# Half of the Strassen activation sums on GpSimd, and one plain tile fewer in the second half layer

## The chip, the cores and the metric

The kernel runs on one core of one Trainium2 chip. Its time is the device time of one launch in microseconds (us). A run of the kernel before and one of the changed kernel can be told apart from about 0.2% on, some 3.3 us here.

The engines are named as in the profile: PE is the matrix engine (TensorE), PEld its weight loads, DVE the vector engine (VectorE), ACT the scalar engine (ScalarE), POOL is GpSimd, SP the sync engine, which issues most loads. Each engine works through its own queue of instructions strictly in order, and waits for others at semaphores.

## The reference

One step of a two-layer decoder, in float32, for 512 prompt tokens and 8 sample tokens that share the weights (520 token columns in all), with a model width of 1024 and a feed-forward width of 2816. The first layer mixes tokens with a pooling mixer, the second with windowed attention; around each mixer stand two feed-forward blocks that add half of their output:

```python
def _rmsnorm(x, g):
    y = xf * lax.rsqrt(jnp.mean(xf * xf, axis=-1, keepdims=True) + EPS)
    return (y * g.astype(jnp.float32)).astype(x.dtype)

def _swiglu(x, wg, wu, wd):
    return (jax.nn.silu(x @ wg) * (x @ wu)) @ wd

# every layer: x += 0.5*SwiGLU(rms(x)); x += mixer(rms(x)); x += 0.5*SwiGLU(rms(x))
```

So there are four feed-forward blocks. They are called half layers here and numbered fi = 0 to 3.

## The kernel before

The residual stream lies transposed in SBUF: eight tiles x0 to x7 of 128 model rows by 520 token columns. Every float32 product is formed of three fp32r products (high times high, low times high, high times low), so each weight and each activation is first split into a high and a low part: ACT copies the high part (`wh`, `th`), DVE subtracts it to get the low part (`wl`, `tl`). The token columns are worked in two halves of 260.

A half layer has 22 tiles of 128 hidden columns. Each tile needs gate and up products. A **plain** tile takes 96 matmuls of 128x260 (8 row blocks, 2 weights, 2 halves, 3 products). A **Strassen** tile uses seven block products instead of eight, 84 matmuls; it needs sums of weight blocks and sums of activation blocks. `NPL` says how many tiles of each half layer are plain; they come first and give the sums time to be formed.

The activation sums are formed once for each half layer. For quarter k = 0 to 3, ACT writes the scaled inputs `xa` (from x_k) and `xb` (from x_k+4), in slots of tag "sa". Then four sums of 128x260 are formed on DVE: t1 = b11 - b12, t2 = -t1 - b22, t3 = b22 - b12, t4 = -t2 - b21. t1 and t2 fill the tile `t12`, t3 and t4 the tile `t34` (tag "sb", which other values share). Both tiles are then split: ACT writes `th` (L358), DVE writes `tl` (L359). In fi = 0 and 2 this is the generator `sums()` (L676, L677, L681, L682), and the order of its instructions among the others is set by the framework's scheduler. In fi = 1 and 3 it is `begin()` (t1 to t4 at L839, L841, L843, L845, the splits at L852), and the order is set by the planner `Steps`, which is given an engine, a cost in us and a due time for each step, and the slots that it takes. There t1 to t4 are the steps T{k}1 to T{k}4, the splits H{k}0 and L{k}0 (of t12), H{k}1 and L{k}1 (of t34). The first Strassen product s0 needs no sums; the second, s1, needs all four L{k}0.

The weight sums are two. SP loads a chunk `raw` (1 MB, gate then up, at L372) and one more block into a tile `S`. POOL then issues two accumulating DMAs on its own queue (L157 into `S`, L158 within `raw`), each of which waits until its loads have landed. DVE adds twice more (L163, L167). A chunk slot is loaded again as soon as its last block has been split (L196, L225).

POOL otherwise computes little: the power step of the norm in `begin()` (L805, N.r in the plan), parts of the attention softmax (L1856, L1817), and some DMAs of results.

At the start of each half layer the norm is computed beside the first plain tiles. In fi = 0, ACT squares the eight x tiles into `sq` and DVE adds them into `acc` (L1088); PE sums acc over the rows (L498); DVE computes the reciprocal root `r_tok` by Newton steps (L506 to L513); PE spreads it over the columns (L519, L522); ACT copies it to `R` (L523, L524). The gate values of the plain tiles are multiplied by R afterwards. In fi = 1 and 3 the same steps are N.s (L798), N.m (L802, DVE), N.r (L805, POOL), N.b (L810, L813, PE) and copies at L819.

Of the kernel before, what the change touches and what calls it, by code (L numbers as in the profile page):

```python
# [15 lines left out]
ALU = mybir.AluOpType  # L16
# [11 lines left out]
PARTS = (8, 8, 6)  # L28
LAG = 2
VLAG = 3  # L30
NPL = (3, 3, 2, 2)
HD = 64
NB = SP // P
WINS = (2, 4, 8, 16)
# [211 lines left out]
class Steps:  # L246
# [8 lines left out]
    def add(self, name, eng, cost, due, fn=None, after=(), takes=(), reads=()):  # L255
        self.steps[name] = (eng, cost, due, fn, tuple(after), tuple(takes))
        for key in reads:
            self.readers.setdefault(key, []).append(name)
# [58 lines left out]
def yoco_step(ctx, tc, ins, outs):  # L317
    nc = tc.nc
# [3 lines left out]
    V, S, T = nc.vector, nc.scalar, nc.tensor  # L322
# [41 lines left out]
    def later(ins):  # L364

        return tc.keep_in_program_order(ins)
# [297 lines left out]
    def sums(tmp, n, tt):  # L664


        for k in range(4):
            xa = tmp.tile([P, TOK], F32, tag="sa", name="xa")
            xb = tmp.tile([P, TOK], F32, tag="sa", name="xb")
            for kk, xn in ((k, xa), (k + 4, xb)):  # L670
                S.activation(xn, x[kk], AF.Copy, scale=gcol(n, kk))
            t12 = tmp.tile([P, TOK], F32, tag="sb", name="t12", bufs=nsb[0])
            t34 = tmp.tile([P, TOK], F32, tag="sb", name="t34", bufs=nsb[0])
            b11, b12, b21, b22 = hcols(xa, 0), hcols(xa, 1), hcols(xb, 0), hcols(xb, 1)
            t1, t2, t3, t4 = hcols(t12, 0), hcols(t12, 1), hcols(t34, 0), hcols(t34, 1)
            later(V.tensor_tensor(t1, b11, b12, op=ALU.subtract))  # L676
            V.scalar_tensor_tensor(t2, t1, -1.0, b22, op0=ALU.mult, op1=ALU.subtract)  # L677
            tt[k] = pair(TT, [P, TOK])
            split(tt[k], t12)
            yield  # L680
            later(V.tensor_tensor(t3, b22, b12, op=ALU.subtract))  # L681
            V.scalar_tensor_tensor(t4, t2, -1.0, b21, op0=ALU.mult, op1=ALU.subtract)  # L682
            tt[k + 4] = pair(TT, [P, TOK])
            split(tt[k + 4], t34)
            yield
# [99 lines left out]
    def begin(st, fi, n, mov, tmp, tt, first, off, base, need, ready, summed, hidden_list, root_):  # L785


        add, vals = st.add, {}
# [32 lines left out]
        d = base + root_  # L821
# [11 lines left out]
        def t_sum(k, i):  # L833
            (b11, b12), (b21, b22) = ((hcols(vals["X", k, a], 0), hcols(vals["X", k, a], 1)) if ("X", k, a) in vals else (None, None) for a in range(2))
            if i in (1, 3):
                vals["t", k, i // 2] = tmp.tile([P, TOK], F32, tag="sb", name="t12" if i == 1 else "t34", bufs=nsb[0])
            h = lambda j: hcols(vals["t", k, (j - 1) // 2], (j - 1) % 2)
            if i == 1:
                V.tensor_tensor(h(1), b11, b12, op=ALU.subtract)  # L839
            elif i == 2:  # L840
                V.scalar_tensor_tensor(h(2), h(1), -1.0, b22, op0=ALU.mult, op1=ALU.subtract)  # L841
            elif i == 3:
                V.tensor_tensor(h(3), b22, b12, op=ALU.subtract)  # L843
            else:
                V.scalar_tensor_tensor(h(4), h(2), -1.0, b21, op0=ALU.mult, op1=ALU.subtract)  # L845

# [7 lines left out]
        for k in range(4):  # L854
            d = S0 - 14.0 + 3.0 * k
            add(f"X{k}0", "ACT", 0.72, d, lambda k=k: scaled(k, 0), after=ready(k) + ([f"X{k - 1}1"] if k else []), takes=("sa",))
            add(f"X{k}1", "ACT", 0.72, d, lambda k=k: scaled(k, 1), after=ready(k + 4) + [f"X{k}0"], takes=("sa",))
            x0, x1 = ("sa", f"X{k}0"), ("sa", f"X{k}1")
            add(f"T{k}1", "DVE", 0.43, d + 0.5, lambda k=k: t_sum(k, 1), after=[f"X{k}0"], takes=("sb",), reads=[x0])
            add(f"T{k}2", "DVE", 0.43, d + 1.0, lambda k=k: t_sum(k, 2), after=[f"X{k}1", f"T{k}1"], reads=[x1])  # L860
            add(f"T{k}3", "DVE", 0.43, d + 1.1, lambda k=k: t_sum(k, 3), after=[f"X{k}1", f"X{k}0"], takes=("sb",), reads=[x0, x1])
            add(f"T{k}4", "DVE", 0.43, d + 1.2, lambda k=k: t_sum(k, 4), after=[f"T{k}2", f"T{k}3"], reads=[x1, ("sb", f"T{k}1")])
            for u, src in ((0, 1), (1, 3)):
                e = d + 1.5 + (0.5 if u == 0 else 4.0)
                add(f"H{k}{u}", "ACT", 0.65, e, lambda k=k, u=u: t_hi(k, u), after=[f"T{k}{src + 1}"] + ([f"H{k - 1}{u}"] if k else []))
                add(f"L{k}{u}", "DVE", 0.7, e + 0.3, lambda k=k, u=u: t_lo(k, u), after=[f"H{k}{u}"], reads=[("sb", f"T{k}{src}")])
# [19 lines left out]
        for p in range(npl):  # L886
# [4 lines left out]
            for q, (k, o) in enumerate(order):  # L891
                i = off + 4 * p + 2 * (k // 4) + o
                after = [f"wl{i}"] + need(k) + ([prev] if prev else [f"p{p - 1}.71"] if p else [])
# [3 lines left out]
                    takes=("d",) if k == 0 else (), reads=[("w", f"wh{i}")] if k % 4 == 3 else [],  # L897
                )
            d = P0(p + 1)
# [4 lines left out]
                reads=[("d", f"p{p}.01"), ("t", f"S{p}")],  # L904
# [28 lines left out]
        for q in range(6):  # L933
            add(
                f"s{q}", "PE", 1.44, S0 + 1.44 * q, run[q], after=[f"wl{i0 + q}"] + extra[q],
                takes=("d",) if q < 2 else (), reads=[("w", f"wh{i0 + q}")],
# [1471 lines left out]
```

## Time and profile before

| what | us |
|---|---|
| median of 3 runs | 1651.93 (1651.38 to 1654.89) |
| the profiled execution, its time | 1651.43 |
| the profiled execution, its span | 1649.7 |
| PE busy in it | 1635.1 (99%) |
| DVE busy | 1241.2 (75%) |
| ACT busy | 877.0 (53%) |
| POOL busy | 178.2 (11%) |
| granted PE clock | 0.998 |

The span runs from the first to the last instruction of the profiled execution; 1.7 us of its time lie around it. PE is busy for nearly all of the span, so the time can change in two ways: by the number of matmuls, and by gaps in which PE waits. Line numbers such as L676 are lines of the kernel file. In a timeline row the columns are the start in us from the span's start, the length in us, engine, line, operation, and "output<-input" by the tile names of the program; x2 means that two instructions are joined in the row, and brackets give the idle time before it and what ended it.

### The profile page before, as it was taken

Reading aid. Unit: us, or ns where it says so; the run is one execution under the profiler, and the core shown is the slowest. Engines: PE = TensorE matmul, PEld = TensorE weight load, DVE = VectorE, ACT = ScalarE, POOL = GpSimd, SP = SyncE. Lnnn points to the kernel's source line nnn. Section 1 sums busy time; section 2 is a strip of 40 time slices with the busy share of each in tenths; the row PEclk is TensorE's granted clock in tenths of the full one; section 3 lists DMA queues with packets and bytes.
Section 4 is the critical chain, followed back from the end, with each engine's and each line's share of the span. In section 5 each row is a group of like instructions: output and inputs, shape, how many; then the busy total and the mean of one; then the engine's idle time right before and its main releaser. Section 6 shows DMA issues by size and latency. Waiting matters only on the chain.

```text
span 1649.7 us, 34525 instructions
## 1 busy us (share of the span) xinstructions
PE 1635.1 (99%) x13814; PEld 1620.5 (98%) x13814; DVE 1241.2 (75%) x2351; ACT 877.0 (53%) x1756; POOL 178.2 (11%) x236
## 2 busy tenths in 40 slices
PE   9999999999999999999999999999999999999997
PEld 9999999999999999999999999999989999999997
DVE  7966875878775875878784785778997785785786
ACT  6643643666652652556562552555875662563463
POOL 1101101001101101100201101100220110110100
PEclk9999999999999999999999999999999999999999
DMA  9546845761655765633756665654142566665641
GB/s 244 135 120 136 175 141 137 164 204 54 149 153 134 167 160 135 154 109 97 169 153 155 131 165 152 139 150 114 27 104 65 129 154 166 140 156 149 128 121 52
DMA packets 317423, 226.28 MB, mean 137 GB/s; under 512 B 9520, under 2 KB 292776, under 8 KB 317222
## 3 DMA queue, kind: packets, MB, share of 16 engines
q1 hardware_dynamic: 290832, 178.24, 38.7%
q0 software_dynamic: 23104, 41.31, 15.9%
q10 hardware_dynamic: 3326, 4.53, 0.9%
q8 instruction: 108, 1.77, 0.4%
q14 instruction: 53, 0.43, 0.1%
HBM read 180.63 MB, written 5.04 MB: 113 GB/s over the span
## 4 chain that ended last, share of the span: by engine, by line
PE 97%; DVE 1%; ACT 0%; DMA 0%; issue 0%; SPq 0%; DVEq 0%; ACTq 0%
PE ps L560 48%; PE ps L534 36%; PE pa L534 5%; PE ps L2203 2%; PE ps L1378 1%; PE pb L1808 1%; PE p L534 1%; PE pc L1879 1%; PE pc L1864 1%; PE ps L1415 1%; DMA raw<-in_ffn_w_gate_dram 0%; PE ps L2244 0%; DVE wl L225 0%; PE t L1066 0%; DVE sm L1827 0%; PE ps L498 0%
## 5 line engine op out<-in xcount | busy, mean ns | idle before, releaser
L195 ACT ACTIVATE wh<-raw 128x512 fp32r<-128x512 f32 (+1 forms) x658 | 397.9, 622 | 482.2 <-PE ps L534 285.8
L196 DVE TENSOR_TENSOR wl<-raw,wh 128x512 fp32r<-128x512 f32 (+1 forms) x658 | 434.8, 677 | 176.3 <-ACT wh L195 172.7
L560 PE MATMUL ps<-th,wh 128*128 128x260 f32 x1248 | 352.1, 283 | 1.0 <-DVE sb L653 0.8
L560 PE MATMUL ps<-tl,wh 128*128 128x260 f32 x1248 | 352.4, 282 | 0.0
L560 PE MATMUL ps<-th,wl 128*128 128x260 f32 x1248 | 350.9, 282 | 0.0
L560 PEld LDWEIGHTS ps<-th,wh 128*128 128x128 f32 x1248 | 234.5, 188 | 1.5 <-DVE sb L653 1.0
L560 PEld LDWEIGHTS ps<-tl,wh 128*128 128x128 f32 x1248 | 234.7, 188 | 0.0
L560 PEld LDWEIGHTS ps<-th,wl 128*128 128x128 f32 x1248 | 234.3, 188 | 0.0
L534 PE MATMUL ps<-hh,wh 128*128 128x260 f32 x1024 | 206.5, 283 | 0.6 <-ACT vtok L1630 0.6
L534 PE MATMUL ps<-hl,wh 128*128 128x260 f32 x1024 | 207.0, 282 | 0.0
L534 PE MATMUL ps<-hh,wl 128*128 128x260 f32 x1024 | 205.1, 282 | 0.0
L560 PE MATMUL ps<-xh,wh 128*128 128x260 f32 x696 | 195.0, 282 | 0.6 <-ACT sb L643 0.6
L560 PE MATMUL ps<-xl,wh 128*128 128x260 f32 x696 | 194.9, 282 | 0.0
L560 PE MATMUL ps<-xh,wl 128*128 128x260 f32 x696 | 191.6, 282 | 0.0
L158 POOL DMA_DIRECT2D raw<-raw x78 | 69.2, 887 | 1068.8 <-DVE wl L196 446.0
L534 PEld LDWEIGHTS ps<-hl,wh 128*128 128x128 f32 x1024 | 158.3, 188 | 0.0
L534 PEld LDWEIGHTS ps<-hh,wh 128*128 128x128 f32 x1024 | 157.1, 188 | 0.9 <-ACT vtok L1630 0.9
L534 PEld LDWEIGHTS ps<-hh,wl 128*128 128x128 f32 x1024 | 157.4, 188 | 0.0
L728 DVE TENSOR_TENSOR u<-ps,R 128x520 f32<-128x520 f32 x86 | 60.0, 698 | 98.0 <-PE ps L534 98.0
L560 PEld LDWEIGHTS ps<-xh,wh 128*128 128x128 f32 x696 | 130.8, 188 | 0.8 <-ACT sb L643 0.8
L560 PEld LDWEIGHTS ps<-xl,wh 128*128 128x128 f32 x696 | 131.1, 188 | 0.0
L534 PE MATMUL ps<-xl,wh 128*128 128x260 f32 x640 | 130.2, 283 | 0.0
(339 smaller groups left out, 3297.2 us busy)
## 6 DMA issues: line engine op xcount, KB each, us to landing
raw<-in_ffn_w_gate_dram SPq DMA_DIRECT2D x87, 512.0 KB
raw<-in_ffn_w_up_dram SPq DMA_DIRECT2D x87, 512.0 KB
raw<-in_ffn_w_down_dram SPq DMA_DIRECT2D x32, 1024.0 KB
S<-in_ffn_w_up_dram SPq DMA_DIRECT2D x78, 256.0 KB
raw<-raw POOLq DMA_DIRECT2D x78, 256.0 KB, 3.4
S<-raw POOLq DMA_DIRECT2D x78, 256.0 KB, 4.8
raw<-in_ffn_w_down_dram SPq DMA_DIRECT2D x16, 768.0 KB
raw<-in_w_q_dram SPq DMA_DIRECT2D x8, 512.0 KB
```

Source lines behind the costliest of these rows:

```text
L158: G.dma_start(blk(raw, 2, 1), blk(raw, 1, 1), accum_op=ALU.add)
L195: nc.scalar.activation(dh, src, AF.Copy)
L196: nc.vector.tensor_tensor(dl, src, dh.bitcast(F32), op=ALU.subtract)
L534: T.matmul(banks[:, hf, :H], a[:, kk, :], hcols(b, hf), start=(first and i == 0), stop=(last and i == 2),)
L560: T.matmul(bank[:, :H], a[:, kk, :], b, start=(not more and kk == 0 and i == 0), stop=(kk == 3 and i == 2), skip_group_check=more,)
L728: V.tensor_tensor(halves(u), banks[m][:, :, :H], halves(R), op=ALU.mult)
L1378: T.matmul(o, a[:, s], b[:, kk, :], start=(n == 0), stop=(n == 5))
L1415: T.matmul(o, za, b, start=(i == 0), stop=(i == len(lst) - 1))
L1808: T.matmul(o, q_[rows_, qc], k_[rows_, kc_], start=(i == 0), stop=(i == 2))
L1864: T.transpose(pt[:, o : o + P], vals["sm", t, h, bi][:, e, kt * P : (kt + 1) * P], ident)
L1879: T.matmul(po[rows_, bi * P : (bi + 1) * P], vtok[:, max(b - 1, 0) + kt, v0 : v0 + 64], vals["pp", t, h, bi][:, kt * 256 + e * P : kt * 25 ...
L2203: T.matmul(bank, a[:, k % 3, :], b[:, c0:c1], start=(k == 0 and i == 0), stop=(k == 5 and i == 2))
```

## The change

Two edits. First, t1 and t3 of every quarter move from DVE to POOL in all four half layers: 4 quarters x 2 sums x 4 half layers = 32 instructions of 128x260. In `Steps` their cost is given as 1.6 instead of 0.43. Second, the half layer fi = 1 has two plain tiles instead of three, and one Strassen tile more.

```diff
-NPL = (3, 3, 2, 2)
+NPL = (3, 2, 2, 2)
 ...
-            later(V.tensor_tensor(t1, b11, b12, op=ALU.subtract))
+            later(nc.gpsimd.tensor_tensor(t1, b11, b12, op=ALU.subtract))
 ...
-            later(V.tensor_tensor(t3, b22, b12, op=ALU.subtract))
+            later(nc.gpsimd.tensor_tensor(t3, b22, b12, op=ALU.subtract))
 ...
             if i == 1:
-                V.tensor_tensor(h(1), b11, b12, op=ALU.subtract)
+                nc.gpsimd.tensor_tensor(h(1), b11, b12, op=ALU.subtract)
 ...
             elif i == 3:
-                V.tensor_tensor(h(3), b22, b12, op=ALU.subtract)
+                nc.gpsimd.tensor_tensor(h(3), b22, b12, op=ALU.subtract)
 ...
-            add(f"T{k}1", "DVE", 0.43, d + 0.5, lambda k=k: t_sum(k, 1), after=[f"X{k}0"], takes=("sb",), reads=[x0])
+            add(f"T{k}1", "POOL", 1.6, d + 0.5, lambda k=k: t_sum(k, 1), after=[f"X{k}0"], takes=("sb",), reads=[x0])
 ...
-            add(f"T{k}3", "DVE", 0.43, d + 1.1, lambda k=k: t_sum(k, 3), after=[f"X{k}1", f"X{k}0"], takes=("sb",), reads=[x0, x1])
+            add(f"T{k}3", "POOL", 1.6, d + 1.1, lambda k=k: t_sum(k, 3), after=[f"X{k}1", f"X{k}0"], takes=("sb",), reads=[x0, x1])
```

Both the scheduler and the planner then order the whole neighbourhood anew. Three places show it. Tile numbers tell the quarters and chunks apart.

First, POOL in fi = 0. L158 and L157 are the accumulating weight DMAs, raw_369, raw_424 and raw_575 the first three Strassen chunks. Before:

```order
L158 DMA raw_369<-raw_369 128x512
L157 DMA S<-raw_369 128x512
L158 DMA raw_424<-raw_424 128x512
L158 DMA raw_575<-raw_575 128x512
L157 DMA S<-raw_424 128x512
L157 DMA S<-raw_575 128x512
```

Now:

```order
L158 DMA raw_369<-raw_369 128x512
L157 DMA S<-raw_369 128x512
L676 TENSOR_TENSOR t_459<-xa 128x260
L681 TENSOR_TENSOR t_460<-xb,xa 128x260
L676 TENSOR_TENSOR t_557<-xa 128x260
L681 TENSOR_TENSOR t_558<-xb,xa 128x260
L158 DMA raw_424<-raw_424 128x512
L676 TENSOR_TENSOR t_663<-xa 128x260
L681 TENSOR_TENSOR t_664<-xb,xa 128x260
L676 TENSOR_TENSOR t_710<-xa 128x260
L158 DMA raw_575<-raw_575 128x512
L681 TENSOR_TENSOR t_711<-xb,xa 128x260
```

The sums of quarters 0 and 1 stand behind the DMAs of the first chunk, those of quarter 2 and t1 of quarter 3 behind the DMA of raw_424, and t3 of quarter 3 behind the DMA of raw_575.

Second, DVE in fi = 0, where it works on the last sums of squares for the norm. Before:

```order
L225 TENSOR_TENSOR wl<-raw_128,wh 128x512
L1088 TENSOR_TENSOR acc<-acc,sq 128x520
L225 TENSOR_TENSOR wl<-raw_128,wh 128x512
L1088 TENSOR_TENSOR acc<-acc,sq 128x520 x2
L196 TENSOR_TENSOR wl<-raw_131,wh 128x512 x2
L676 TENSOR_TENSOR t_459<-xa 128x260
```

Now:

```order
L225 TENSOR_TENSOR wl<-raw_128,wh 128x512
L677 SCALAR_TENSOR_TENSOR t_459<-t_459,xb 128x260
L1088 TENSOR_TENSOR acc<-acc,sq 128x520
L225 TENSOR_TENSOR wl<-raw_128,wh 128x512
L1088 TENSOR_TENSOR acc<-acc,sq 128x520
L682 SCALAR_TENSOR_TENSOR t_460<-t_459,xb 128x260
L196 TENSOR_TENSOR wl<-raw_131,wh 128x512
L1088 TENSOR_TENSOR acc<-acc,sq 128x520
```

The sum t2 (L677), which needs POOL's t1, now stands ahead of the last three additions into acc. Somewhat later in the same queue the last Newton steps (L510 to L513) stand among the sums and splits of quarter 3 now:

```order
L677 SCALAR_TENSOR_TENSOR t_710<-t_710,xb 128x260
L196 TENSOR_TENSOR wl<-S,wh 128x512
L511 SCALAR_TENSOR_TENSOR nt<-nt,nv 128x5
L682 SCALAR_TENSOR_TENSOR t_711<-t_710,xb 128x260
L513 SCALAR_TENSOR_TENSOR ny<-nt,ny 128x5
L359 TENSOR_TENSOR tl<-t_710,th 128x520
L510 TENSOR_TENSOR nt<-ny 128x5
L359 TENSOR_TENSOR tl<-t_711,th 128x520
L511 SCALAR_TENSOR_TENSOR nt<-nt,nv 128x5
L196 TENSOR_TENSOR wl<-raw_369,wh 128x512
L513 SCALAR_TENSOR_TENSOR r_tok<-nt,ny 128x5
```

Before, all Newton steps came ahead of quarters 1 to 3. On PE the row sums L498 moved behind 8 matmuls, and the spread L519 stands 88 matmuls behind L498 instead of 56.

Third, POOL in the planned half layers. In fi = 3 it was, around the norm's power step L805:

```order
L157 DMA S<-raw_16908 128x512
L158 DMA raw_16908<-raw_16908 128x512
L805 TENSOR_TENSOR r_tok<-nv,minus_half 128x5
L158 DMA raw_17367<-raw_17367 128x512
L157 DMA S<-raw_17071 128x512
```

and is now:

```order
L157 DMA S<-raw_16922 128x512
L158 DMA raw_16922<-raw_16922 128x512
L839 TENSOR_TENSOR t_17168<-xa 128x260
L805 TENSOR_TENSOR r_tok<-nv,minus_half 128x5
L843 TENSOR_TENSOR t_17209<-xb,xa 128x260
```

t1 of quarter 0 stands ahead of the power step. In fi = 1 it is now:

```order
L843 TENSOR_TENSOR t_5591<-xb,xa 128x260
L158 DMA raw_5603<-raw_5603 128x512
L157 DMA S<-raw_5462 128x512
L158 DMA raw_5462<-raw_5462 128x512
L157 DMA S<-raw_5603 128x512
L839 TENSOR_TENSOR t_5662<-xa 128x260
L843 TENSOR_TENSOR t_5685<-xb,xa 128x260
```

where before POOL had only the DMAs. Four weight DMAs stand ahead of t1 and t3 of quarter 3.

## The prediction

> **What bounds the kernel now.** I read the page's busy line and its chain first.
>
> ```profile
> PE 1635.1 (99%) x13814; PEld 1620.5 (98%) x13814; DVE 1241.2 (75%) x2351; ACT 877.0 (53%) x1756; POOL 178.2 (11%) x236
> PE 97%; DVE 1%; ACT 0%; DMA 0%; issue 0%; SPq 0%; DVEq 0%; ACTq 0%
> ```
>
> PE is busy for 99% of the span and 97% of the chain. DVE, which the change relieves, has a quarter of its time free. So taking 32 instructions from DVE buys nothing by itself, and only fewer matmuls or fewer PE waits can gain. Next the list of what PE waits for. These entries lie where the change reorders work:
>
> ```profile
> PE ps L534 <- ACT vtok L1630: 0.6, 1, 0.6
> PE ps L560 <- ACT sb L643: 0.6, 1, 0.6
> ```
>
> The first is in fi = 2, the second at the first Strassen tiles of fi = 0. Together with a few tenths beside them, about 2 us of waits could vanish. The question is what the new queue orders add, so I read stretch by stretch what stands in line on POOL and DVE.
>
> **What a sum costs on POOL.** No sum of this shape runs there now. The nearest rows, by form, and one overlap:
>
> ```profile
> L676 DVE TENSOR_TENSOR t<-xa x8: 420/424/431, 30.1 to 790.5; 128x260 f32<-128x260 f32 x8
> L1856 POOL TENSOR_SCALAR sm<-sm,den 128x256 f32<-128x256 f32 x8 | 9.3, 1167 | 14.8 <-DVE den L1849 14.7
> L1856 POOL TENSOR_SCALAR sm<-sm,den 128x128 f32<-128x128 f32 x8 | 6.6, 826 | 30.1 <-DVE den L1849 30.0
> 1201.84 1.60 POOL L1856 TENSOR_SCALAR sm<-sm,den 128x256 f32<-128x256 f32 x1 [3.54 <-DVE den L1849]
> 1202.05 1.49 DVE L225 TENSOR_TENSOR wl<-raw,wh 128x512 fp32r<-128x512 f32 x2
> ```
>
> 128 columns cost 0.83 us and 256 cost 1.17 on POOL with one tile as input, so 260 would cost about 1.18. A sum reads two streams, and an instruction of 256 columns took 1.60 beside two splits on DVE. I take T = 1.4, between 1.18 and 1.60. The bounds: twice DVE's 0.42, 0.85, below; and 2.2 above, which is what the power step of fi = 3 takes in a crowded stretch (its row is below).
>
> [...]
>
> **The plain tile.** A Strassen tile has 84 matmuls instead of 96. These PE rows in fi = 0 give the cadence:
>
> ```profile
> 30.95 1.28 PE L498 MATMUL ps<-ones,acc 128*128 128x1 f32 x10
> 32.09 0.48 PE L534 MATMUL ps<-xh,wh 128*128 128x260 f32 x2
> 38.88 1.05 PE L519 MATMUL ps<-ident,r_tok 128*128 128x128 f32 x8
> 39.92 0.49 PE L534 MATMUL ps<-xl,wh 128*128 128x260 f32 x2
> ```
>
> 56 matmuls stand between 32.09 and 38.88, or 0.121 us each. Twelve fewer save **1.45 us**. The additional weight sums, splits and DMAs lie beside PE work: DVE is idle for 25% of the span and ACT for 47%, and the chunk DMAs run ahead of their use. I cost them at nothing; uncovered, one late split of 128x512 would be 0.6.
>
> **fi = 0, the row sums.** POOL and DVE there:
>
> ```profile
> 26.98 1.18 POOL L157 DMA_DIRECT2D S<-raw  x1
> 26.31 0.70 DVE L1088 TENSOR_TENSOR acc<-acc,sq 128x520 f32<-128x520 f32 x1 [0.48 <-ACT sq L1084]
> 26.93 0.68 DVE L225 TENSOR_TENSOR wl<-raw,wh 128x512 fp32r<-128x512 f32 x1
> 27.53 1.50 DVE L1088 TENSOR_TENSOR acc<-acc,sq 128x520 f32<-128x520 f32 x2
> ```
>
> t1 of quarter 0 stands on POOL behind the DMA of 26.98, which ends at 28.16. So t1 ends at 28.16 + 1.4 = 29.56. On DVE, t2 (L677) waits for it ahead of the three additions that ran from 26.31 to 29.03 before. From 29.6 DVE needs t2 0.34, an addition 0.62, the split 0.6, an addition 0.6, t4 0.34, a split 0.6 and the last addition 0.7 (starts of neighbouring rows): it ends at 33.4. PE reaches L498 eight matmuls later than before, at 31.9. It waits until 33.45: **+1.5 us**, where before it had 1.9 us of slack.
>
> **fi = 0, the spread.** L519 now stands 88 matmuls behind L498: 33.45 + 1.14 + 88 x 0.121 = 45.25. It needs r_tok, whose last steps stand on DVE behind the sums and splits of quarter 3, which wait for POOL, which waits for two chunk DMAs, which wait for loads. The links:
>
> ```profile
> 28.05 0.90 SPq L372 DMA_DIRECT2D raw<-in_ffn_w_up_dram  x1
> 36.76 0.85 POOL L158 DMA_DIRECT2D raw<-raw  x1 [8.60 <-DVE r_tok L513]
> 31.89 0.68 DVE L196 TENSOR_TENSOR wl<-raw,wh 128x512 fp32r<-128x512 f32 x1
> 33.02 1.32 SPq L372 DMA_DIRECT2D raw<-in_ffn_w_up_dram  x1
> 40.70 0.85 POOL L158 DMA_DIRECT2D raw<-raw  x1 [3.09 <-DMA S<-in_ffn_w_up_dram]
> 58.55 0.58 SPq L372 DMA_DIRECT2D raw<-in_ffn_w_up_dram  x1
> 64.45 0.85 POOL L158 DMA_DIRECT2D raw<-raw  x1 [21.12 <-DVE wl L196]
> 36.32 0.16 DVE L513 SCALAR_TENSOR_TENSOR r_tok<-nt,ny 128x5 f32<-128x5 f32 x1
> 37.39 0.72 ACT L671 ACTIVATE xa<-x,gT 128x520 f32<-128x520 f32 x1
> 39.23 0.64 ACT L358 ACTIVATE th<-t 128x520 fp32r<-128x520 f32 x1
> ```
>
> From the second load of a chunk to POOL's DMA it takes 8.7, 7.7 or, later, 5.9 us. Raw_424 is loaded once the split of 26.93 is through, now 30.56 to 31.24, so its second load goes out at 31.7 and POOL's DMA at 37.6 to 40.4. The transfers that crowded it before are older then; I take 38.2. Its 0.85, t1 and t3 of quarter 2 (2.8), `xa` of quarter 3 on ACT (0.7, it needs the slot that t3 reads) and t1 of quarter 3 (1.4) end at 44.0. Raw_575 is loaded after the split that ended at 32.57 and now follows t2 of quarter 1. DVE goes on from the additions at 33.35 and has four splits of 0.6 ahead of that t2, so it comes there at 35.75. Its t1 is done by then (t3 of quarter 0 from 30.65, behind an addition, to 32.05, `xa` to 32.8, t1 to 34.25). With t2 0.34 and 0.68 the split ends at 36.8, the second load goes at 37.25 and POOL's DMA at 43.1 to 45.0. I take 44.05, after t1. Then 0.85 and t3 (1.4) to 46.3, `th` 0.64, `tl` 0.6, a Newton step 0.2, a split 0.6, the last step 0.2: r_tok stands at 48.65. PE waits **+3.4 us**; before, r_tok stood at 36.48, 2.4 us ahead of L519.
>
> Behind L522 the next matmuls now need R at once; before, 28 stood between. R is copied by ACT up to here:
>
> ```profile
> 40.58 0.17 ACT L524 COPY R<-ps 128x8 f32<-128x8 f32 x1
> ```
>
> That is 1.87 after L519 began (38.88), and PE goes on 1.04 after it: **+0.9**, with the semaphore. Sum for fi = 0: +5.8. The 4 us of delay give ACT and DVE time for the sums, and the wait for `sb` should go: of the 2 us above I credit **-1.0**. In fi = 2 the sums stand behind chunk DMAs too, which ran here:
>
> ```profile
> 780.26 0.86 POOL L158 DMA_DIRECT2D raw<-raw  x1 [86.73 <-DVE t L677]
> 791.62 0.86 POOL L158 DMA_DIRECT2D raw<-raw  x1 [10.49 <-DVE t L677]
> 796.01 0.88 POOL L158 DMA_DIRECT2D raw<-raw  x1 [1.56 <-DMA raw<-in_ffn_w_up_dram]
> ```
>
> But the Newton steps of fi = 2 stand ahead of all its sums on DVE now, and the three sums between the first two DMAs take 4.2 of the 11.4 us there. I put it at nothing; if the last pair, behind two more DMAs, came late for s1, it would cost what those take, 1 to 2 us.
>
> **fi = 1 and fi = 3.**
>
> ```profile
> 413.96 0.48 PE L534 MATMUL ps<-xh,wh 128*128 128x260 f32 x2
> 421.11 0.94 POOL L157 DMA_DIRECT2D S<-raw  x1 [9.38 <-DMA S<-in_ffn_w_up_dram]
> 421.76 1.18 POOL L158 DMA_DIRECT2D raw<-raw  x1
> 410.48 1.25 POOL L805 TENSOR_TENSOR r_tok<-nv,minus_half 128x5 f32<-128x5 f32 x1 [12.94 <-DVE nv L802]
> 1284.50 1.23 POOL L158 DMA_DIRECT2D raw<-raw  x1
> 1285.08 2.23 POOL L805 TENSOR_TENSOR r_tok<-nv,minus_half 128x5 f32<-128x5 f32 x1
> 1287.37 1.16 PE L810 MATMUL ps<-ident,r_tok 128*128 128x128 f32 x8
> ```
>
> fi = 1: with two plain tiles, 90 matmuls are left at 413.96, so s0 starts at 424.9 and s1 at 426.3. Four DMAs stand on POOL ahead of t1 of quarter 3. The loads of this place let the DMAs start at 421.1 before; now one more is ahead of that and one behind, so the last ends near 423.3. t1 ends at 424.7 and t3 at 426.1; on DVE t4 (0.4), a split (0.6) and the `tl` that s1 needs (0.7) follow: 427.8. **+1.5 us** (0 to 3).
>
> fi = 3: the power step ended at 1287.31, and PE's spread L810 began at 1287.37, with no slack. Now t1 of quarter 0 stands ahead: the DMA ends at 1285.73, t1 at 1287.13, the power step (1.25 alone) at 1288.4: **+1.1 us** (0.5 to 1.9).
>
> **The sum:** 1651.43 - 1.45 - 1.0 + 5.8 + 1.5 + 1.1 = **1657.4 us**, 0.4% above the profiled execution. The median lies 0.5 above it; I leave the forecast as it is.
>
> **The rivals.** *Cheap sums* (not slower). With T = 0.85 the same steps give: L498 waits 1.0, r_tok comes at 46.55 against 44.7 (1.85), R 0.9, fi = 1 0.4, fi = 3 0.55. 1651.43 - 2.45 + 4.7 = 1653.7, which a measurement cannot tell from no change. It decides below T of about 1.0, or where the loads of raw_424 and raw_575 land early. For it: a bare two-fold of DVE's time. Against: every POOL row above.
>
> *Crowded sums.* POOL and DVE hinder each other throughout, T = 2.2: L498 waits 2.3, r_tok comes at 52.6 against 46.05 (6.5), R 0.9, fi = 1 3.1, fi = 3 1.9: 1663.7. For it: 2.23 at 1285.08. Against: part of that 2.23 is the DMA ahead of it, and DVE idles while it waits for t1.
>
> *All hidden* (faster). If PE's spread did not wait at all, only 1.45 and at most 2 us of waits count: 1648.3. The queue orders speak against it.
>
> *Starved weights.* The extra Strassen tile of fi = 1 leaves its chunks no lead and costs 2 us more: 1659.4. Against: the chunk DMAs run far ahead of their use in the other half layers.
>
> **How the numbers follow.** Forecast 0.46, cheap sums 0.29, crowded sums 0.18, starved weights 0.04, all hidden 0.03. A measurement of this kernel tells 0.2% (3.3 us) from no change: faster needs 1648.6, slower 1655.2. Forecast, crowded and starved are slower: 0.68; cheap sums 0.29; faster 0.03. The forecast's own range is 1655 to 1660; with the bounds of T it is 1652 to 1663.
>
> **What would show it.** Right: a PE gap of 1 to 2 us before L498 near 32, one of 2 to 5 before L519 near 45, about 1 behind L522, gaps of about 1 before L810 in fi = 3 and before s1 in fi = 1; POOL rows L676 and L681 of 1.2 to 1.6 us. Wrong: no gap before L519 (the loads were early, or the steps are not reached in this order), sums under 1 us, or gaps inside the later Strassen tiles, which would speak for starved weights.

## The result and the profile after

| | before | after |
|---|---|---|
| median of 6 runs each, us | 1651.66 (1650.50 to 1654.89) | 1661.90 (1660.39 to 1667.90) |
| the profiled execution, its time, us | 1651.43 | 1665.32 |
| its mean granted PE clock | 0.998 | 0.993 |

The ratio is **1.0070, 95% interval 1.0058 to 1.0082**: slower by some 10 us, where 6.0 were forecast (1657.4 against 1651.43). The executions differ by more than those of before, and the longest have the lowest mean clocks: 0.994 to 0.996 in the four of 1660.39 to 1662.07, 0.993 and 0.992 in those of 1665.32 and 1667.90. The profiled one is among the longer: it is 13.9 above before's profiled one.

The page's busy line and its chain:

```profile
PE 1639.4 (99%) x13802; PEld 1624.2 (98%) x13802; DVE 1245.0 (75%) x2327; ACT 881.7 (53%) x1762; POOL 206.9 (12%) x270
PE 89%; DVE 5%; DMA 2%; issue 1%; ACT 1%; POOL 1%; SPq 0%; DVEq 0%; ACTq 0%; POOLq 0%
```

PE has 12 matmuls fewer, as the edit of `NPL` says, and yet is busy for 4.3 us *longer* (1639.4 against 1635.1). At 0.12 us a matmul the tile should have taken 1.45 off, so the matmuls that are left took 5.8 us more in sum. The span grew by 13.9; 13.9 - 4.3 = 9.6 us is PE standing still. So the difference has three parts: **+9.6 waits, -1.45 tile, +5.8 slower matmuls**. DVE has 24 instructions fewer and is busy for 3.8 us longer.

What PE waits for, the entries that before did not have (total, times, longest):

```profile
PE ps L519 <- DVE r_tok L513: 2.5, 1, 2.5
PE ps L534 <- DVE g L617: 2.3, 1, 2.3
PE ps L498 <- DVE acc L1088: 2.3, 1, 2.3
PE ps L560 <- DVE tl L852: 1.9, 2, 1.4
PE ps L534 <- ACT R L524: 0.7, 1, 0.7
```

They sum to 9.7. The two waits of before that the prediction quotes are gone (1.2 us). Of the 1.1 us that are missing to 9.6, the wait for the first `xh` near the start has 0.6 (1.0 instead of 0.4 in this view; it is 1.3 in the run without any sums on POOL, npl_only, so it is not theirs); the rest lies in gaps of a few tenths.

The slower matmuls show in windows of 1 us (columns: stretch, length, busy time of PE, PEld, DVE, ACT and POOL with their instructions, granted clock, DMA share, GB/s):

```profile
10.00:11.00 1.00, 1.00 (x7) 1.00 (x6) 0.98 (x2) 0.00 (x0) 0.00 (x0) 0.50 1.14 294
...
36.00:37.00 1.00, 1.00 (x7) 1.00 (x6) 1.00 (x3) 0.04 (x1) 0.46 (x1) 0.50 0.00 0
...
39.00:40.00 1.00, 1.00 (x9) 1.00 (x8) 0.99 (x5) 0.88 (x2) 0.00 (x0) 0.83 0.47 88
...
54.00:55.00 1.00, 1.00 (x6) 1.00 (x6) 0.91 (x3) 0.84 (x3) 0.00 (x0) 0.50 0.00 0
...
805.00:806.00 1.00, 1.00 (x7) 1.00 (x6) 0.34 (x1) 0.00 (x0) 1.00 (x3) 0.50 1.15 274
```

For four stretches before PE's last matmul the granted clock is 0.50, and PE, where it is busy, shows 5 to 7 matmuls in a microsecond (those that lie partly in it count too) where it shows 10 or 11 at full clock. The first is 8.6 to 12.0, close to the start, and is no part of the loss: before's PE shows as few matmuls there (7, 6 and 7 from 10 to 13), and at 13.4 after is 0.75 us *ahead* of before at the same matmul. The others are 35.9 to 39.3, 49.6 to 56.4 and 803.9 to 807.3. Each begins within 2.3 us of the end of one of the three longest waits of the list above, and half of their busy time is lost: 1.7, 3.0 and 1.7, or 6.4 us. That the 5.8 above are less fits with after's faster start, but the two were not reconciled to the tenth. The page's row of the clock, 42 us to a slice, shows 9, that is 90% or more, everywhere.

### The profile page after: what moved, and what is told of

It reads as the page before. It is cut to its first block, busy times and chain, and to the rows that moved or that the text cites. A ratio compares the mean times of both kernels' runs of the same rounds, so it can differ in the third digit from the quotient of the medians.

```text
span 1663.6 us, 34544 instructions
## 1 busy us (share of the span) xinstructions
PE 1639.4 (99%) x13802; PEld 1624.2 (98%) x13802; DVE 1245.0 (75%) x2327; ACT 881.7 (53%) x1762; POOL 206.9 (12%) x270
## 3 DMA queue, kind: packets, MB, share of 16 engines
q8 instruction: 108, 1.77, 0.4%
## 4 chain that ended last, share of the span: by engine, by line
PE 89%; DVE 5%; DMA 2%; issue 1%; ACT 1%; POOL 1%; SPq 0%; DVEq 0%; ACTq 0%; POOLq 0%
PE ps L560 46%; PE ps L534 30%; PE pa L534 5%; PE ps L2203 2%; PE pb L1808 1%; PE pc L1879 1%; PE pc L1864 1%; DVE wl L196 1%; PE ps L1415 1%; DMA pr<-in_bands_dram 1%; PE ps L1378 1%; DMA raw<-in_ffn_w_up_dram 0%; DMA S<-raw 0%; DVE wl L225 0%; DMA S<-in_ffn_w_up_dram 0%
## 5 line engine op out<-in xcount | busy, mean ns | idle before, releaser
L196 DVE TENSOR_TENSOR wl<-raw,wh 128x512 fp32r<-128x512 f32 (+1 forms) x664 | 442.2, 682 | 183.1 <-ACT wh L195 180.0
L560 PE MATMUL ps<-tl,wh 128*128 128x260 f32 x1264 | 356.8, 282 | 1.9 <-DVE tl L852 1.9
L560 PE MATMUL ps<-th,wh 128*128 128x260 f32 x1264 | 357.4, 283 | 0.9 <-DVE sb L653 0.9
L560 PE MATMUL ps<-th,wl 128*128 128x260 f32 x1264 | 355.1, 282 | 0.0
L158 POOL DMA_DIRECT2D raw<-raw x79 | 70.2, 888 | 1047.3 <-DVE wl L196 448.5
L560 PE MATMUL ps<-xh,wh 128*128 128x260 f32 x708 | 198.6, 283 | 0.0
L560 PE MATMUL ps<-xl,wh 128*128 128x260 f32 x708 | 198.3, 282 | 0.0
L560 PE MATMUL ps<-xh,wl 128*128 128x260 f32 x708 | 195.0, 282 | 0.1
L560 PEld LDWEIGHTS ps<-xh,wl 128*128 128x128 f32 x708 | 131.4, 188 | 0.3 <-DVE wl L225 0.3
```

The lines of the kernel that those rows point to most:

```text
L158: G.dma_start(blk(raw, 2, 1), blk(raw, 1, 1), accum_op=ALU.add)
L196: nc.vector.tensor_tensor(dl, src, dh.bitcast(F32), op=ALU.subtract)
L560: T.matmul(bank[:, :H], a[:, kk, :], b, start=(not more and kk == 0 and i == 0), stop=(kk == 3 and i == 2), skip_group_check=more,)
```

## Where the waits come from

fi = 0, the timeline of after at the places of the prediction's steps:

```profile
27.34 1.35 POOL L676 TENSOR_TENSOR t<-xa 128x260 f32<-128x260 f32 x1
28.73 0.43 DVE L677 SCALAR_TENSOR_TENSOR t<-t,xb 128x260 f32<-128x260 f32 x1 [3.64 <-POOL t L676]
30.29 1.25 DVE L1088 TENSOR_TENSOR acc<-acc,sq 128x520 f32<-128x520 f32 x1
32.40 1.23 DVE L1088 TENSOR_TENSOR acc<-acc,sq 128x520 f32<-128x520 f32 x1
33.68 1.05 PE L498 MATMUL ps<-ones,acc 128*128 128x1 f32 x8 [2.26 <-DVE acc L1088]
36.54 0.87 POOL L158 DMA_DIRECT2D raw<-raw  x1 [1.72 <-DMA raw<-in_ffn_w_up_dram]
46.05 1.03 POOL L681 TENSOR_TENSOR t<-xb,xa 128x260 f32<-128x260 f32 x1
49.51 0.16 DVE L513 SCALAR_TENSOR_TENSOR r_tok<-nt,ny 128x5 f32<-128x5 f32 x1
49.72 2.08 PE L519 MATMUL ps<-ident,r_tok 128*128 128x128 f32 x8 [2.54 <-DVE r_tok L513]
52.77 0.80 PE L534 MATMUL ps<-xh,wh 128*128 128x260 f32 x2 [0.74 <-ACT R L524]
```

The chain is the one that the prediction follows: t1 behind two DMAs on POOL, t2 behind it on DVE, the additions into acc behind t2, and so L498; then the last t3 behind a DMA that waits for loads, the Newton steps behind the sums of quarter 3, and so L519 and R. What it did not have: two of the additions take 1.25 and 1.23 us beside POOL's sums where the third took 0.69. Also, the eight matmuls of L519 take 2.08 instead of 1.05, for the granted clock was 0.50 there.

fi = 2:

```profile
797.46 0.87 POOL L158 DMA_DIRECT2D raw<-raw  x1 [5.17 <-DVE t L682]
798.05 1.18 POOL L157 DMA_DIRECT2D S<-raw  x1
798.62 1.37 POOL L681 TENSOR_TENSOR t<-xb,xa 128x260 f32<-128x260 f32 x1
800.02 0.73 ACT L671 ACTIVATE xa<-x,gT 128x520 f32<-128x520 f32 x1 [2.31 <-POOL t L681]
...
801.38 0.98 DVE L359 TENSOR_TENSOR tl<-t,th 128x520 fp32r<-128x520 f32 x1 [2.94 <-ACT th L358]
802.28 0.68 DVE L617 TENSOR_TENSOR g<-ps,R 128x520 f32<-128x520 f32 x1
803.02 0.51 PE L534 MATMUL ps<-hh,wh 128*128 128x260 f32 x2 [2.29 <-DVE g L617]
```

A t3 stands on POOL behind the two DMAs of a chunk and ends at 799.99. On ACT the next `xa` waits for it, and behind that stands the `th` of the same t34; on DVE `tl` waits for `th`; and behind `tl` stand the gate values `g` (L617), by which PE is released at 803.02. `g` uses no sum: it is late only because it stands behind one in DVE's queue.

fi = 1, where t1 of quarter 3 stands on POOL behind four DMAs (of 429.56 to 431.56):

```profile
432.14 1.77 POOL L839 TENSOR_TENSOR t<-xa 128x260 f32<-128x260 f32 x1
...
437.71 0.39 PE L560 MATMUL ps<-tl,wh 128*128 128x260 f32 x1 [1.36 <-DVE tl L852]
```

And the sums by form, which are the forecast's T:

```profile
L843 POOL TENSOR_TENSOR t<-xb,xa 128x260 f32<-128x260 f32 x8 | 9.5, 1191 | 2.4 <-ACT xb L831 2.4
...
L681 POOL TENSOR_TENSOR t<-xb,xa 128x260 f32<-128x260 f32 x8 | 7.9, 985 | 4.1 <-ACT xb L671 2.3 <-DVE acc L1088 1.9
```

Between these lie L839 and L676. A sum takes 0.99 to 1.19 us in the mean, less than the 1.4 that the forecast took.

## The experiments

All ratios are to runs of the kernel before on the same chip; those runs had medians of 1651.4 to 1652.8.

| kernel | median, us | ratio, 95% interval |
|---|---|---|
| only `NPL` (npl_only) | 1650.81 | 0.9990, 0.9977 to 1.0003 |
| `NPL`, sums on POOL in fi = 0 (pool_fi0) | 1659.32 | 1.0042, 1.0030 to 1.0054 |
| `NPL`, sums on POOL in fi = 2 (pool_fi2) | 1653.37 | 1.0009, 0.9997 to 1.0021 |
| `NPL`, sums on POOL in fi = 1 and 3 (pool_fi13) | 1654.76 | 1.0016, 1.0004 to 1.0027 |
| that, two sums of fi = 1 back on DVE (k3_on_dve) | 1654.10 | 1.0007, 0.9996 to 1.0019 |
| all sums on POOL, `NPL` as before (pool_only) | 1664.41 | 1.0078, 1.0061 to 1.0095 |
| before, the root of fi = 1 three times (root_x3) | 1653.67 | 1.0015, 1.0005 to 1.0024 |
| four times (root_x4) | 1658.34 | 1.0035, 1.0022 to 1.0048 |
| five times (root_x5) | 1659.33 | 1.0050, 1.0032 to 1.0069 |
| four times, PE kept busy (root_x4_fill) | 1655.11 | 1.0022, 1.0012 to 1.0031 |
| after, sums of fi = 0 written behind the norm (norm_first) | 1661.08 | 1.0063, 1.0044 to 1.0083 |
| and held behind it by their data (norm_held) | 1657.54 | 1.0036, 1.0024 to 1.0049 |

### The parts by themselves

npl_only is the kernel before with the one line; the three others add the move of the sums in some half layers (`n` is 0 in fi = 0 and 3 in fi = 2).

```diff
-NPL = (3, 3, 2, 2)
+NPL = (3, 2, 2, 2)
 # pool_fi0; pool_fi2 has n == 3; t3 likewise
-            later(V.tensor_tensor(t1, b11, b12, op=ALU.subtract))
+            later((nc.gpsimd if n == 0 else V).tensor_tensor(t1, b11, b12, op=ALU.subtract))
```

> Only the tile swap: fi = 1 has two plain tiles, all activation sums stay on DVE. Theory (the cost of the change lies in the queue orders that the POOL sums bring, the swap is worth its 12 matmuls): 1.45 us less than before, about 1650.2, and no new PE wait over 0.5 us in fi = 1. Rival (the extra Strassen tile starves its weights): no gain or up to 2 us more, 1651.7 to 1653.7, with PE waits for wl or S near 430 to 450.

> The tile swap, and the POOL sums in fi = 0 alone. Theory A (waits plus the granted clock): the waits before L498 (2.3), L519 (2.5) and behind L522 (0.7) come again, and PE runs some 3 us at half clock after each of the first two and after the third: 1651.7 - 1.45 - 1 + 5.5 + 3 to 5 = 1657.8 to 1659.8. Rival B (waits alone, the clock is noise of that execution): 1651.7 - 1.45 - 1 + 5.5 = 1654.8 and no half clock in the windows behind the waits.

> The tile swap, and the POOL sums in fi = 2 alone. Theory A: one wait of about 2.3 us at the first matmul behind the transposes (gate value L617 behind a split that waits for POOL's t3, which stands behind two weight DMAs), 0.8 of old waits gone, and about 3.2 us at half clock behind it, 1.6 lost: 1651.7 - 1.45 + 2.3 - 0.8 + 1.6 = 1653.3. Rival B (no clock term): 1651.8.

> The tile swap, and the POOL sums in the planned half layers fi = 1 and 3. Theory: fi = 1 waits 1.4 for the last split before s1 (four weight DMAs ahead of t1 of quarter 3 on POOL), fi = 3 waits 0.5 at L810, 0.5 to 0.9 at s1, and under 1 more in its first Strassen tiles; all these waits are under 2 us, so the clock stays full: 1651.7 - 1.45 + 1.5 + 2.5 = 1654.2, and no window at half clock there. Rival (POOL and DVE hinder each other everywhere): 1657 or more, with DVE late in the later Strassen tiles too.

The tile alone gives -1.1 us, about the -1.45 that it was costed at, though its interval takes in no change. Against it the sums cost 8.5 us in fi = 0, 2.6 in fi = 2 and 3.9 in fi = 1 and 3 together. With the tile that makes +13.9 where the whole change has +10.2; the four intervals, some 2 us each way, hold that difference. So the loss is the sums', mostly in fi = 0, and none of it that can be measured the tile's. In npl_only's trace PE gains 0.6 us in fi = 1 and not 1.45: waits of a few tenths near 437 to 440 and one near 476 take the rest. pool_only says the same of the sums from the other side: without the tile it is no faster than the whole change. Its median, 1664.41, lies above the 1661 to 1663 that were expected (its interval reaches down to 1661.7); the wait of 1.4 in fi = 1 is gone, as expected.

> The POOL sums in all half layers without the tile swap. Theory: the swap is worth about 1 us, and the third plain tile of fi = 1 gives its sums 11.6 us more, so that the wait of 1.4 before s1 there goes: within 1 us of the changed kernel, 1661 to 1663, with the waits of fi = 0 and fi = 2 and none over 0.5 in fi = 1. Rival (the tile swap and the sums hinder each other): 1658 or less.

PE's waits in pool_fi0 and one window behind each; then the same for pool_fi2; then the wait of pool_fi13:

```profile
33.99 0.72 PE L498 MATMUL ps<-ones,acc 128*128 128x1 f32 x5 [2.69 <-DVE acc L1088]
36.00:37.00 1.00, 1.00 (x6) 1.00 (x6) 1.00 (x3) 0.00 (x0) 0.10 (x1) 0.50 0.00 0
49.79 1.16 PE L519 MATMUL ps<-ident,r_tok 128*128 128x128 f32 x8 [2.34 <-DVE r_tok L513]
50.00:51.00 1.00, 1.00 (x10) 0.98 (x9) 0.96 (x2) 0.00 (x0) 0.00 (x0) 1.00 1.04 178
```

```profile
792.83 0.51 PE L534 MATMUL ps<-hh,wh 128*128 128x260 f32 x2 [1.92 <-DVE g L617]
794.00:795.00 1.00, 1.00 (x6) 1.00 (x6) 0.06 (x1) 0.03 (x1) 0.72 (x2) 0.50 1.13 226
```

```profile
423.42 1.78 POOL L839 TENSOR_TENSOR t<-xa 128x260 f32<-128x260 f32 x1
429.01 0.39 PE L560 MATMUL ps<-tl,wh 128*128 128x260 f32 x1 [1.21 <-DVE tl L852]
```

Each part brings its own waits of after with it. In pool_fi0 the wait of 2.69 is followed by half clock and the one of 2.34 is not: this profiled execution took 1656.48, the shortest of the eight, and the longest took 1662.56. (Why the wait of 2.34 escaped is worked out in the last section.) In pool_fi2 a wait of 1.92 halved the clock. In fi = 1 and 3 no wait reaches 1.3 us and the clock stays at 1.00.

### What a wait costs: the root three, four and five times

To price a wait of PE by itself, the kernel before gets no sums on POOL at all, but repeats the power step N.r in fi = 1, for which PE waits at its spread (L810, one line later here):

```diff
-            nc.gpsimd.tensor_tensor(r_tok[:, :5], vals["v"], minus_half, op=ALU.pow)
+            for _ in range(4 if fi == 1 else 1):
+                nc.gpsimd.tensor_tensor(r_tok[:, :5], vals["v"], minus_half, op=ALU.pow)
```

> The kernel before, with the power step of the norm in fi = 1 done three times over on POOL (the same value each time), so that PE's spread L810 waits. From the rows of before (power step 410.48 to 411.73, L810 at 412.93 unhindered): a wait of about 1.3 us. Theory A (the clock halves only after a wait of more than about 2 us): +1.3 us, full clock. Rival B (any wait costs its length alone): the same here; the pair with the next two runs tells them apart.

> The same with four power steps: a wait of about 2.5 us. Theory A: +2.5 and some 3.2 us at half clock behind it, 1.6 lost: +4.1 us, with windows at 0.50. Rival B: +2.5 and full clock. As the clock seems to be set in steps of a fixed time, single executions may escape it.

> The same with five power steps: a wait of about 3.8 us. Theory A: +3.8 + 1.6 to 2.2 = +5.4 to 6.0 us, half clock behind it. Rival B: +3.8.

The row of the wait, and one window some 3 us behind it, of each in this order:

```profile
415.52 1.16 PE L811 MATMUL ps<-ident,r_tok 128*128 128x128 f32 x8 [1.48 <-POOL r_tok L806]
418.00:419.00 1.00, 1.00 (x10) 1.00 (x9) 1.00 (x3) 1.00 (x4) 0.00 (x0) 1.00 1.21 289
```

```profile
415.24 2.08 PE L811 MATMUL ps<-ident,r_tok 128*128 128x128 f32 x8 [2.73 <-POOL r_tok L806]
418.00:419.00 1.00, 1.00 (x6) 1.00 (x6) 0.73 (x2) 1.00 (x4) 0.00 (x0) 0.50 0.49 115
```

```profile
416.02 2.08 PE L811 MATMUL ps<-ident,r_tok 128*128 128x128 f32 x8 [3.97 <-POOL r_tok L806]
418.00:419.00 1.00, 1.00 (x7) 1.00 (x7) 0.00 (x0) 0.64 (x3) 0.00 (x0) 0.50 0.06 14
```

A wait of 1.48 costs its length: PE is 1.56 us later behind the place than in before. A wait of 2.73 costs 5.7, and one of 3.97 costs 6.4: in both the clock is halved from 414 to 421, which takes some 3 us more. So the step from 1.5 to 2.7 us of waiting is worth 4 us and the next 1.2 us of waiting worth under 1. That the half clock is the cause, and not the late root, the fourth run tells: it has the same fourfold root, and PE gets 22 idle-filling matmuls of 128x260 ahead of the spread, whose result the spread overwrites.

```diff
+            for _ in range(22 if fi == 1 else 0):
+                T.matmul(pr[:, :H], mov[0][0][:, :P], mov[0][0][:, :H], start=True, stop=True)
```

> The kernel with four power steps in fi = 1 (there PE waits 2.9 us before L810 and then runs at half clock for two stretches of 3.4 us, +6.9 us in all), and 22 matmuls of 128x260 put in front of the spread, whose result the spread writes over. They take 22 x 0.12 = 2.66 us, in which PE would have waited. Theory A (PE's idleness lowers the clock): the spread starts as late as without them, but the clock stays full: +2.7 to 3.2 us against the kernel before, 1654.4. Rival B (the delay itself, through late splits or the late R, costs the rest): +5 to +7, 1657 to 1658.

```profile
411.96 2.78 PE L811 MATMUL ps<-xh 128*128 128x260 f32 x22
414.85 1.16 PE L813 MATMUL ps<-ident,r_tok 128*128 128x128 f32 x8
418.00:419.00 1.00, 1.00 (x11) 1.00 (x10) 1.00 (x3) 1.00 (x3) 0.00 (x0) 1.00 0.33 77
```

The spread comes as late as in root_x4 (414.85 against 415.24), the clock stays at 1.00, and PE is 2.8 us later behind the place instead of 5.7. Its median is 3.2 us below that of root_x4, by doing more work; the intervals of the two ratios overlap, so it is the trace that decides here.

### fi = 0: is it the order on DVE?

norm_first is the changed kernel with the sums of fi = 0 written behind the steps of the norm; norm_held also makes the scaled inputs depend on `r_tok` (their scale is copied by DVE behind it), so that no sum can start before the root is done.

```diff
 # norm_first (no step() inside norm() any more)
-            return [step, norm, two, norm_all, two, step, step]
+            return [none, norm, none, norm_all, two, two, two, two]
 # norm_held in addition; held() is called behind the root
+    def held():
+        for i in (0, 4):
+            V.scalar_tensor_tensor(g0[:, i : i + 4], r_tok[:, :4], 0.0, gT[:, i : i + 4], op0=ALU.mult, op1=ALU.add)
-                S.activation(xn, x[kk], AF.Copy, scale=gcol(n, kk))
+                S.activation(xn, x[kk], AF.Copy, scale=gcol(n, kk) if n else g0[:, kk : kk + 1])
```

> The changed kernel, with all sums of fi = 0 emitted behind the norm instead of around it. All POOL sums are still there. Theory A (the order puts the norm behind POOL): the wait before L498 is gone and its half clock too; t2 of quarter 0 still stands ahead of the last Newton steps and waits for POOL behind raw_424's DMA, so L519 waits up to 2 us: 3 to 7 us less than the change, 1655 to 1659. Rival (POOL's sums and their contention with DVE cost the time wherever they stand): within 1 us of the change, 1661 to 1663.

> The changed kernel, with the sums of fi = 0 made to depend on r_tok: the scaled inputs take their scale from a copy that DVE writes behind the last Newton step (the same values). All sums stay on POOL. Theory (the norm must not stand behind POOL): no wait before L498, none before L519, no half clock there. The last quarters then come late for s1: POOL has quarter 1 behind three weight DMAs, near 44, and 2.9 us for each further quarter, so s1 at 52 waits 1 to 2.5 us. fi = 0 costs 1 to 4 us instead of 8.5: 1654 to 1658. Rival (POOL sums in fi = 0 cost the same wherever they stand, as in the run with the norm emitted first): 1661 to 1662.

norm_first gained nothing that can be told apart, against its expectation. Its rows say why:

```profile
36.99 1.06 POOL L676 TENSOR_TENSOR t<-xa 128x260 f32<-128x260 f32 x1
38.08 0.95 DVE L677 SCALAR_TENSOR_TENSOR t<-t,xb 128x260 f32<-128x260 f32 x1 [5.96 <-POOL t L676]
...
42.63 1.65 PE L519 MATMUL ps<-ident,r_tok 128*128 128x128 f32 x6 [4.46 <-DVE r_tok L513]
```

The wait before L498 is gone, but the scheduler put the first t2 among the Newton steps all the same. DVE stands still for 5.96 us behind it, because POOL's t1 is now behind the DMA of the second chunk. One wait of 4.46 and half clock took the place of two waits. In norm_held neither L498 nor L519 waits, and its median is 3.5 us below that of norm_first (their intervals just overlap, 1.0044 and 1.0049). But the sums run late into the first Strassen products: ACT's weight splits `wh` stand behind a split of a sum and a scaled input, and PE waits for them:

```profile
54.58 0.39 PE L560 MATMUL ps<-xh,wh 128*128 128x260 f32 x1 [1.86 <-ACT wh L195]
56.00:57.00 1.00, 1.00 (x6) 1.00 (x6) 1.00 (x3) 0.64 (x1) 0.00 (x0) 0.50 0.00 0
```

So DVE's order was the cause of the waits at L498 and L519. Putting it right takes about half of fi = 0's loss away: by where PE stands behind fi = 0 in the traces, counted from 14 us on, the loss is 6.7 in pool_fi0, 7.5 in pool_only and 9.2 in after, 6.4 in norm_first, and 4.4 in norm_held. The other half returns behind the norm, in the first Strassen products.

### fi = 1: is it POOL's queue?

```diff
-                nc.gpsimd.tensor_tensor(h(1), b11, b12, op=ALU.subtract)
+                (V if fi == 1 and k == 3 else nc.gpsimd).tensor_tensor(h(1), b11, b12, op=ALU.subtract)
 # t3 likewise, and in the plan their engine and cost
```

> This is the kernel with the first layer's row moved and the sums on GpSimd in the half layers 1 and 3, with two sums of half layer 1 (those of the fourth quarter's tiles 1 and 3) back on VectorE. In the run with both on GpSimd TensorE waited about 1.5 us near 427.5 us for a tile sum whose GpSimd part stood in the queue behind four weight loads issued from 420.86 to 424.4 us; that run took 1654.8. Theory (the wait comes from the queue ahead of the GpSimd sum): the wait of over 1 us in half layer 1 is gone, the waits at the end of half layer 3 stay (about 1.5 us in all), and the time is 1653.3, 1652.5 to 1654. Rival (VectorE's own work or the splits are late there, whoever forms the sums): a wait of over 1 us stays in half layer 1 before the first product of the new quarter, and the time stays at 1654.8.

```profile
420.16 0.42 DVE L839 TENSOR_TENSOR t<-xa 128x260 f32<-128x260 f32 x1
```

There is no wait over 0.2 us left in fi = 1 before the first new quarter product, with t1 of quarter 3 on DVE at 420.16 instead of on POOL at 423.42. So the wait came from the queue of four DMAs ahead of the sum. By the traces this is worth 0.6 us and not the 1.2 of the row: about half a microsecond comes back as a wait near 476, which npl_only has too. The times of the two cannot be told apart, and 1654.10 lies at the upper end of the range expected. The waits of fi = 3 stay, as the theory had it.

## Why the prediction was right in sign and short in size

- **The sum, its form.** "Only fewer matmuls or fewer PE waits can gain": each wait entered with its own length. That is the step that failed. A wait of PE of some 2 us or more here mostly cost its length and then a stretch of 3.4 or 6.8 us at half clock, in which matmuls took twice as long (2.08 instead of 1.05 for the eight of L519): 1.7 or up to 3.4 us on top. In the profiled execution this came three times behind the new waits. Of the 13.9 us there, 6.0 were forecast; of the 7.9 that are missing, 5.8 are slower matmuls, for which the sum has no term, and the other 2.1 are about the wait of 2.29 in fi = 2, which was put at nothing. The runs root_x3 to root_x4_fill show the half clock apart from any sum. Even before's trace held a sign of it, which was not read: behind PE's last matmul its clock falls to 0.50 within two microseconds.

```profile
1643.00:1644.00 1.00, 0.21 (x2) 0.00 (x0) 0.35 (x2) 0.65 (x2) 0.68 (x1) 1.00 0.00 0
1645.00:1646.00 1.00, 0.00 (x0) 0.00 (x0) 0.26 (x1) 0.00 (x0) 0.00 (x0) 0.50 0.63 240
```

- **fi = 0, the row sums:** +1.5 forecast, 2.26 measured, on the chain that was named. Two errors nearly cancel in it: POOL's t1 ended at 28.69 and not at 29.56, but DVE's additions beside POOL's sums took 0.55 us longer each, twice. So the last addition ended at 33.63, where 33.4 was put. The rest of the difference is PE, which was ready for L498 at 31.3 to 31.4 and not at 31.9, since it was ahead from the start.
- **fi = 0, the spread:** +3.4 forecast at 45.25, 2.54 measured from 47.2; R +0.9 forecast, 0.74 measured. The two waits and R sum to 5.5 where 5.8 were put, and that nearness is partly luck. POOL's DMA of raw_424 went out earlier than taken (36.54, not 38.2), but that of raw_575 later (45.44, not 44.05), and r_tok stood at 49.67, 1.0 us *later* than forecast. The wait is shorter only because PE came to L519 1.9 us later than forecast, most of it (1.7) for the half clock behind the first wait.
- **fi = 1:** +1.5 forecast, 1.36 measured, from the DMAs on POOL as said; k3_on_dve shows it. Its net worth there is smaller, 0.6.
- **fi = 2:** put at nothing, with 1 to 2 us if late for s1. It cost 2.29 and half clock behind it, at another place: the gate values L617, queued on DVE behind a `tl` that hangs on POOL's t3. The prediction named what waits for the sums, but not what is queued behind them.
- **fi = 3:** +1.1 forecast at L810. It was not there. In the new order L810 stands 30 matmuls behind the row sums L798 instead of 24, which is 0.7 us more, and the power step ends 0.5 us later after their start than before, not 1.1. So PE does not wait:

```profile
1299.28 1.05 PE L810 MATMUL ps<-ident,r_tok 128*128 128x128 f32 x8
1319.64 0.39 PE L560 MATMUL ps<-tl,wh 128*128 128x260 f32 x1 [0.49 <-DVE tl L852]
```

  Instead the Strassen tiles wait several times for short spans between 1319 and 1371; from their start to the next part PE takes 108.6 us instead of 106.1. So 2.5 us, in a place that "gaps inside the later Strassen tiles" came near to. The waits list names a releaser for two of these gaps only, `tl` (L852) and, at 1370, `sb` (L653); the cause of the others stays open.
- **The tile:** -1.45 forecast, -1.1 measured (not told from none; 0.6 by the trace of npl_only). **The old waits:** -1.0 credited; both entries are gone, 1.2 us.
- **T:** 1.4 taken, 0.99 to 1.19 measured, and up to 1.77 right behind DMAs. No run shows the 0.85 of *cheap sums*, twice DVE's 0.42, as a mean: it was the author's estimate, and the means measured are 2.3 to 2.8 times 0.42. The rival *cheap sums* was said to decide below T of about 1.0; T came out near that border, below the forecast, and the time above both, because of the clock and fi = 2. *Crowded sums* is near in time (1663.7) for another reason; its T of 2.2 was not seen. *Starved weights* and *all hidden* were not seen either. Two small sums of the prediction do not come out as written, and nothing hangs on them: *all hidden* gives 1648.0 and not 1648.3, and the bounds of T give 1653.7 to 1663.7, where 1652 to 1663 is put.

## What to carry to other kernels

Don't price a wait on a matrix engine that is otherwise never idle by its length alone: in these runs, among long matmuls, waits of 1.21 to 1.7 us cost no more than about their length (1.48 in root_x3 cost 1.56); those of 1.9 and more mostly cost 1.7 to 3.4 us on top. So the shorter ones were the cheap ones here, and in the trace even useless matmuls that filled a long one paid (2.8 us in root_x4_fill, 5.7 in root_x4). When a cheap instruction moves to an engine whose queue also issues transfers that wait for loads, follow the transfers ahead of it on its new queue, and then every instruction queued behind those that wait for it on the old one; those behind need not use the sum at all. A mean busy share (DVE 75%) says nothing about either.

## What the runs showed of the chip that was not expected

- **The granted clock of PE fell to 0.50 after most waits of about 2 us or more.** Of PE's waits (by the rows' brackets), those of 1.21, 1.36 and 1.48 did not bring it, nor did two of 1.7 (in norm_first at L617, in norm_held in fi = 1); those of 1.86 (with short gaps around it), 1.92, 2.26, 2.29, 2.54, 2.69, 2.73, 3.00 (pool_only at L498), 3.97 and 4.46 did; and one of 2.34 (pool_fi0) and one of 2.17 (pool_only, at L617) did not. Half clock began as much as 2.2 us behind the end of the wait (33.68 to 35.92 in after).
- **The clock changed on a grid, and PE's idle time within one field, that is one step, of it told which waits brought half clock.** By the mean clock of the windows, after's clock changes at 8.62, 12.02, 35.92, 39.34, 49.58, 56.40, 803.92 and 807.34. The shortest distances are 3.40 to 3.42 us, and all come out as whole multiples of 3.413: the 27.30 from 8.62 to 35.92 is 8 of them, the 754.34 from 49.58 to 803.92 is 221. This grid, laid over the traces, accounts for both exceptions. In pool_fi0 the clock changes at 35.56, so a field ends at 49.21, in the middle of the wait of 2.34: 1.76 us of idle time fall before it and 0.58 behind. In pool_only a change at 34.18 puts a border at 798.77, and the wait of 2.17 has about 1.0 before it and 1.2 behind. In after the waits of 2.54 and 2.29 put 2.39 and 2.29 us into one field, and the next one runs at half clock. Among long matmuls (25 to 1600 us, all traces) no field at full clock with up to 1.76 us of idle time was followed by half clock, and each with 1.91 or more was. Where very short matmuls fill the rest of a field, less was enough: 1.17 beside 1.05 us of L498's one-column matmuls in after, and 1.28 at the start of after, beside eight matmuls of 8 columns.
- **The place of the grid differs from trace to trace.** The traces, each of another kernel, have a change at 35.92 in after, 35.56 in pool_fi0 and 34.18 in pool_only, so the wait of 2.29 fell into one field in after and that of 2.34 into two in pool_fi0. Whether this is what makes the executions of one kernel differ was not followed up execution by execution.
- **Some of DVE's work took longer beside POOL's sums.** Additions of 128x520 took 1.25 and 1.23 instead of 0.69 beside a sum on POOL, and the sums themselves up to 1.77 right behind DMA issues, where the quickest took 0.73 (norm_first). DVE's busy time rose by 3.8 us although it lost 24 instructions.
